# Adding the residual in the middle steps of the second product, longer last steps, and activations in DRAM by token quarters

## The chip, the cores and the metric

The kernel runs on one core of a Trainium2 chip, as one launch. The metric is the device time of that launch in microseconds (us). A core has TensorE (PE, matrix products; PEld is its weight load), VectorE (DVE), ScalarE (ACT), GpSimd (POOL) and SyncE (SP), which here issues every DMA, in one queue and in order. Each engine works through its own list of instructions in order; semaphores tie the lists together. SBUF is the on-chip memory with 128 partitions, PSUM holds the results of TensorE, and tensors in DRAM are reached by DMA only.

## The reference, cut to what matters

```python
D_MODEL = SEQ = 1024; D_FF = 4096; ALPHA = 2 ** 0.25

def reference(x, w_in, b_f, pool_w, pool_scale, w_out, ln1_g, ln1_b, w_mlp1, w_mlp2, ln2_g, ln2_b):
    mix = hybrid_mixer(x, w_in, b_f, pool_w, pool_scale, w_out)    # untouched by the change
    x = layer_norm(ALPHA * x + mix, ln1_g, ln1_b)                  # "x1" below
    hid = jnp.square(jax.nn.relu(x @ w_mlp1))                      # first product
    return layer_norm(ALPHA * x + hid @ w_mlp2, ln2_g, ln2_b)      # second product, residual, norm

def layer_norm(x, g, b):
    mu = jnp.mean(x, axis=-1, keepdims=True)
    var = jnp.mean(jnp.square(x - mu), axis=-1, keepdims=True)
    return (x - mu) * lax.rsqrt(var + 1e-5) * g + b
```

All values are float32. Each factor is split into a high and a low part (float32r), and a product takes three matmuls (high by high, high by low, low by high).

## The kernel before, in words

The mixer comes first, then `x1`: eight tiles of 128 tokens by 1024, normed by `norm` on VectorE and stored to `x1_dram`. Both products of the MLP then use the Strassen-Winograd scheme: with each matrix cut into two by two blocks, seven block products `p1` to `p7` stand for eight.

**First product.** Sixteen units (`class Unit`), each two blocks of 128 hidden columns. A unit runs its seven products, each 12 matmuls of 128x128 by 512, in the order p1, p2, p6, p5, p7, p3, p4; VectorE and ScalarE form the relu squares and the sums that the second product needs as its left factors, seven blocks with the names A12, A11, S1, S2, S3, S4, A22. `out` (L655) splits a block into high and low, and stores both to `hid_dram`, whose layout is `[unit, partition, high/low, 7 blocks, 512 tokens]`: a block lies there with its 512 tokens (of one half of the sequence) in a row.

**Second product.** The sixteen units are now the contraction. A step (`class Step`) takes one quarter `q = s % 4` of the 512 tokens of each half, and some consecutive units: step `s` takes the units s-3 to s that exist, so there are 19 steps, with 1, 2, 3, then thirteen times 4, then 3, 2, 1 units. Each step has seven products, each of three matmuls per unit. Its results are added (`into`, L863 to L869) to two tiles `y[q]` and `y[q + 4]` of 128 tokens by 1024 in SBUF, which stay there for all steps. Since each pair of weight tiles (`class Pair`, from `w2`) is used in four steps in a row, one pair comes in with each step: `load_f` (L780) and `load_g` (L784) load 512 KB each into slots of the tag "S" (three buffers of 4 KB a partition); `split_b`, `sums`, `split_t2`, `split_t13` and `split_t4b` make the seven right factors from them, in slots "B".

**Loads of the second product.** `load` (L846) brings the left factors of a step, a block pair at a time: 256 KB a unit for two blocks, 128 KB for A22. A partition's share of one block and one half (high or low) is 128 numbers, 512 bytes in a row. These land in slots "Q" and "A" (eleven of them turn over). `load_y` (L853) fills `y[q]` and `y[q + 4]` with the two tiles of `x1`, 512 KB each, in each of the first four steps; the first addition to a half of `y` then multiplies by ALPHA as it adds (L867, VectorE).

**Last steps.** From step 15 on, a step finishes its two tiles: `norm` with `by="pool"` has statistics on VectorE, the centring on ScalarE (L508) and the two operations with gamma and beta on GpSimd (L509, L512). In the last step, the first tile uses `by="both"` (L492 on VectorE, L511 on ScalarE, L512 on GpSimd), the second `by="vector"` (L492 and L503, stored half by half at L504).

**Order.** Units and steps stand in one chain. Between two neighbours, the products are interleaved by hand: p1 of the new one, p7 of the old, p2, p3 of the old, p6, p4 of the old, p5. `at(i, place, ...)` puts loads, splits and stores between these products, before product number `place`. The program's text gives priorities; the framework's scheduler then orders each engine's list and SP's queue by when a thing can run in its model, and makes an instruction wait where a buffer of its tag is still in use.

The PSUM banks: `k1` of a step is used in turn by p1, p6, p7 and p4, so each of these waits until `into` has read the one before.

Of the kernel before, what the change touches and what calls it, by code (L numbers as in the profile page):

```python
# [14 lines left out]
P = 128  # L15
S = 1024
# [20 lines left out]
def trunk(ctx, tc, xT, xn, wuqk, wvf, bf, poolw, pscale, wout, g1, b1, w1, w2, g2, b2, out):  # L37
# [418 lines left out]
    hid_dram = dr.tile([NF // 2, P, 2, 7, CH], F32, name="hid_dram")  # L456
    H = KT // 2
    VI = {b: i for i, b in enumerate(("A12", "A11", "S1", "S2", "S3", "S4", "A22"))}
# [15 lines left out]
    def norm(y, gam, bet, store, parts=(), res=None, by="vector"):  # L474

        cols = [slice(0, CH), slice(CH, D)]
        st = small([P, 4, 6], "bns", bufs=2)
        mv, rt = small([P, 2], "mv", bufs=2), small([P, 5], "rt", bufs=2)  # L480
        for i, c in enumerate(cols):
            if parts:
                nc.vector.scalar_tensor_tensor(y[:, c], res[:, c], ALPHA, parts[i], ALU.mult, ALU.add)
            nc.vector.bn_stats(st[:, i], y[:, c])
        nc.vector.bn_aggr(mv, st[:, :2])
        v, s, q, r, n = (rt[:, i : i + 1] for i in range(5))

        nc.scalar.activation(s, mv[:, 1:2], AF.Sqrt, bias=eps_sb, scale=0.25)
        nc.vector.tensor_scalar(v, mv[:, 1:2], EPS, 0.25, ALU.add, ALU.mult)

        def scaled(c):
            nc.vector.scalar_tensor_tensor(y[:, c], y[:, c], mv[:, 0:1], gam[:, c], ALU.subtract, ALU.mult)  # L492

        if by != "pool":
            scaled(cols[0])
        nc.vector.reciprocal(q, s)
        nc.vector.scalar_tensor_tensor(q, q, v, s, ALU.mult, ALU.add)
        nc.vector.reciprocal(r, q)
        if by != "pool":
            scaled(cols[1])  # L500
        if by == "vector":
            for c in cols:
                nc.vector.scalar_tensor_tensor(y[:, c], y[:, c], r, bet[:, c], ALU.mult, ALU.add)  # L503
                nc.sync.dma_start(store[:, c], y[:, c])  # L504
            return
        if by == "pool":
            nc.vector.tensor_scalar(n, mv[:, 0:1], r, -1.0, ALU.mult, ALU.mult)
            nc.scalar.activation(y, y, AF.Identity, scale=r, bias=n)  # L508
            nc.gpsimd.tensor_tensor(y, y, gam, ALU.mult)  # L509
        else:  # L510
            nc.scalar.mul(y, y, r)  # L511
        nc.gpsimd.tensor_tensor(y, y, bet, ALU.add)  # L512
        nc.sync.dma_start(store, y)
# [45 lines left out]
    class Unit:  # L559
# [69 lines left out]
        def p7(self):  # L629
            product(self.b1, self.v["T3"], "S3", False)  # L630

            self.rb = slot("A", [2, CH], F32)
            nc.vector.tensor_tensor(self.rb[:, 1], self.cc[:, 1], self.b1, ALU.subtract)

        def p3(self):
            product(self.b2, self.v["B22"], "S4", False)
            nc.vector.tensor_tensor(self.ra[:, 0], self.b2, self.cc[:, 0], ALU.subtract)
            nc.scalar.activation(self.ra, self.ra, AF.Relu)
            nc.scalar.activation(self.ra, self.ra, AF.Square)

        def p4(self):
            product(self.b1, self.v["T4"], "A22", False)
            nc.scalar.activation(self.rb[:, 0], self.b1, AF.Relu)
            nc.scalar.activation(self.rb[:, 1], self.rb[:, 1], AF.Relu)
            nc.scalar.activation(self.rb, self.rb, AF.Square)
            ra, rb = self.ra, self.rb
            self.sa, self.sb = slot("A", [2, CH], F32), slot("A", [2, CH], F32)
            nc.vector.tensor_tensor(self.sb[:, 0], ra[:, 1], rb[:, 0], ALU.subtract)
            nc.vector.tensor_tensor(self.sa[:, 0], rb[:, 0], rb[:, 1], ALU.subtract)

        def sums_s(self):
            nc.vector.tensor_tensor(self.sa[:, 1], self.sa[:, 0], self.ra[:, 1], ALU.subtract)
            nc.vector.tensor_tensor(self.sb[:, 1], self.ra[:, 0], self.sa[:, 1], ALU.add)

        def out(self, name, x):  # L655

            n, i = x.shape[1], VI[name]
            hi = slot("A", [n, CH])
            nc.scalar.copy(hi, x)  # L659
            nc.vector.tensor_tensor(x, x, hi.bitcast(F32), ALU.subtract)  # L660
            nc.sync.dma_start(hid_dram[self.u, :, 0, i : i + n], hi.bitcast(F32))
            nc.sync.dma_start(hid_dram[self.u, :, 1, i : i + n], x)

        def out_r(self):
            self.out("A12", self.ra)
            self.out("A22", self.rb[:, 1:2])
# [8 lines left out]
    for m in range(4):  # L675
# [13 lines left out]
        for t in (2 * m, 2 * m + 1):  # L689
# [18 lines left out]
            norm(xt, gam, bet, x1_dram[t], yp, xt)  # L708
# [116 lines left out]
    NS = NU + 3  # L825

    class Step:

        def __init__(self, s):
            self.s, self.q = s, s % 4
            self.us = [u for u in range(s - 3, s + 1) if 0 <= u < NU]
            self.first, self.final = s < 4, s >= NS - 4
            self.h = {}

        def load(self, names):

            n, i = len(names), VI[names[0]]
            per = 2 // n * 2 if n == 1 else 2  # L840
            qs = slice(self.q * P, (self.q + 1) * P)
            for a in range(0, len(self.us), per):
                h = slot("Q" if nh[0] % 11 < 8 else "A", [per, 2, n, P])
                nh[0] += 1
                for e, u in enumerate(self.us[a : a + per]):
# [163 lines left out]
```

## Time and profile before

| | |
|---|---|
| median of 3 runs | 1090.63 us (1089.4 to 1091.59) |
| profiled execution, its own time | 1088.95 us |
| its span, first to last instruction | 1087.1 us |
| mean granted TensorE clock | 0.979 |
| bytes moved by DMA | 202.62 MB, mean 186 GB/s |
| matmuls of the first product (L554) | from 420.8 us to about 737 us |
| matmuls of the second product (L859) | from 725.1 us to 1067.9 us |

The times of instructions and of stretches below are from the profiled execution, counted from its first instruction. A row of the windows view gives, for a stretch, the busy time of each engine with its number of instructions, the granted clock of TensorE (1.00 is full speed), the mean busy share of the 16 DMA engines (it can come out above 1, since the records of packets overlap a little) and the rate moved. In the timeline and the chain of waits, a row begins with start and duration; in brackets stands the idle time of the engine before it and what ended it. SPq is SP's queue: its rows are the issuing of a DMA, not the transfer.

### The profile page before, as it was taken

What the parts mean: (1) busy time and instruction counts of PE and PEld (TensorE: products, weight loads), DVE (VectorE), ACT (ScalarE), POOL (GpSimd) and SP (SyncE); (2) the same over time, 40 slices, a digit from 0 to 9 for tenths busy, and PEclk for the clock granted to TensorE, in tenths of its full rate; (3) what the DMA queues carried; (4) which work ended last, traced back from release to release, by engine and by line L of the source; (5) the groups of instructions that cost most, each with busy time, mean ns of one, the idle gap of its engine ahead of it and who ended that gap; (6) DMA issues with size and microseconds to landing.
All of it is one profiled execution on the core that took longest, in us unless ns stands there. A gap on an engine that the chain in (4) does not pass through costs nothing.

```text
span 1087.1 us, 14056 instructions
## 1 busy us (share of the span) xinstructions
PE 1029.6 (95%) x5006; PEld 850.3 (78%) x5006; DVE 776.3 (71%) x1315; ACT 493.9 (45%) x783; POOL 59.9 (6%) x77
## 2 busy tenths in 40 slices
PE   7999999999989999999999999995899999999992
PEld 7988788888768777788888888883688888888881
DVE  3576777777886889698887878786665655555378
ACT  3423565666772315477667666763221212222012
POOL 0000000000000021100000000000000000000046
PEclk9999999999999999999999999997799999999996
DMA  6303211111455522167766667599999888888732
GB/s 214 100 26 115 84 49 50 33 50 49 148 158 168 190 98 78 58 252 271 279 243 244 260 224 288 205 334 335 331 303 279 253 248 245 242 253 255 204 122 116
DMA packets 168181, 202.62 MB, mean 186 GB/s; under 512 B 9832, under 2 KB 131496, under 8 KB 168112
## 3 DMA queue, kind: packets, MB, share of 16 engines
q1 hardware_dynamic: 168112, 201.73, 56.8%
q8 instruction: 39, 0.64, 0.3%
q14 instruction: 30, 0.25, 0.1%
HBM read 130.32 MB, written 71.37 MB: 186 GB/s over the span
## 4 chain that ended last, share of the span: by engine, by line
PE 79%; DVE 10%; DMA 5%; ACT 3%; issue 2%; SPq 1%; DVEq 0%; ACTq 0%
PE s L859 15%; PE s L554 11%; PE pv L859 7%; PE mm L554 7%; PE pt L554 6%; PE pv L554 4%; PE pv L384 3%; PE mm L85 2%; PE mm L83 2%; PE mm L84 2%; PE pt L859 2%; PE mm L859 2%; PE s L85 2%; PE s L83 2%; PE s L84 2%
## 5 line engine op out<-in xcount | busy, mean ns | idle before, releaser
L71 ACT CAST B<-S 128x1024 fp32r<-128x1024 f32 (+1 forms) x94 | 80.5, 868 | 207.7 <-DMA S<-in_w_dram 80.7
L859 PE MATMUL s<-B,Q 128*128 128x512 f32 x564 | 139.2, 396 | 12.7 <-DMA Q<-hid_dram 12.7
L859 PEld LDWEIGHTS s<-B,Q 128*128 128x128 f32 x564 | 107.3, 191 | 36.6 <-issue 11.0
L554 PE MATMUL s<-B,Q 128*128 128x512 f32 x504 | 121.0, 393 | 0.7 <-ACT B L71 0.7
L72 DVE TENSOR_TENSOR B<-S,B 128x1024 fp32r<-128x1024 f32 (+1 forms) x94 | 92.8, 994 | 39.1 <-ACT B L71 38.9
L554 PEld LDWEIGHTS s<-B,Q 128*128 128x128 f32 x504 | 95.6, 190 | 21.5 <-ACT B L71 1.0
L71 ACT CAST Q<-S 128x1024 fp32r<-128x1024 f32 x53 | 55.6, 1050 | 62.7 <-DVE S L685 15.4
L72 DVE TENSOR_TENSOR Q<-S,Q 128x1024 fp32r<-128x1024 f32 x53 | 64.6, 1220 | 24.2 <-ACT Q L71 24.0
L554 PE MATMUL mm<-B,Q 128*128 128x512 f32 x324 | 77.6, 390 | 0.0
L859 PE MATMUL pv<-B,Q 128*128 128x512 f32 x279 | 70.8, 397 | 3.8 <-DVE A L867 1.4
L554 PEld LDWEIGHTS mm<-B,Q 128*128 128x128 f32 x324 | 60.8, 188 | 12.9 <-DVE Q L72 0.4
L554 PE MATMUL pt<-B,Q 128*128 128x512 f32 x288 | 68.7, 389 | 0.0
L660 DVE TENSOR_TENSOR A<-A,A 128x1024 f32<-128x1024 f32 (+1 forms) x64 | 67.0, 1084 | 0.2 <-ACT A L659 0.2
L384 PE MATMUL pv<-A,B 128*128 128x256 f32 x320 | 61.5, 297 | 5.0 <-ACT A L369 3.3
L859 PEld LDWEIGHTS pv<-B,Q 128*128 128x128 f32 x279 | 52.9, 190 | 16.8 <-DVE A L867 1.9
L384 PEld LDWEIGHTS pv<-A,B 128*128 128x128 f32 x320 | 49.1, 188 | 21.4 <-ACT A L369 9.9
L554 PEld LDWEIGHTS pt<-B,Q 128*128 128x128 f32 x288 | 54.1, 188 | 11.2
L659 ACT CAST A<-A 128x1024 fp32r<-128x1024 f32 x64 | 58.8, 942 | 6.9 <-DMA hid_dram<-A 2.6
L370 DVE TENSOR_TENSOR A<-pt,A 128x512 fp32r<-128x512 f32 (+1 forms) x80 | 49.2, 634 | 16.4 <-ACT A L369 15.8
L347 ACT ACTIVATE A<-A,nm 128x128 f32<-128x128 f32 (+3 forms) x64 | 49.8, 777 | 20.4 <-DVE nm L345 20.1
L859 PE MATMUL s<-B,A 128*128 128x512 f32 x204 | 53.3, 403 | 2.3 <-DVE A L869 2.3
L869 DVE TENSOR_TENSOR A<-A,s 128x512 f32<-128x512 f32 x47 | 32.0, 681 | 30.3 <-PE s L859 30.3
(353 smaller groups left out, 2125.2 us busy)
## 6 DMA issues: line engine op xcount, KB each, us to landing
hid_dram<-A SPq DMA_DIRECT2D x96, 512.0 KB
Q<-hid_dram SPq DMA_DIRECT2D x141, 256.0 KB
S<-in_w_dram SPq DMA_DIRECT2D x63, 512.0 KB
A<-hid_dram SPq DMA_DIRECT2D x51, 256.0 KB
hid_dram<-A SPq DMA_DIRECT2D x32, 256.0 KB
S<-in_wuqk_dram SPq DMA_DIRECT2D x12, 512.0 KB
Q<-hid_dram SPq DMA_DIRECT2D x47, 128.0 KB
A<-ncf_dram SPq DMA_DIRECT2D x8, 512.0 KB
```

What stands on the lines that cost most here:

```text
L71: nc.scalar.copy(hi, src)
L72: nc.vector.tensor_tensor(lo, src, hi.bitcast(F32), ALU.subtract)
L83: nc.tensor.matmul(dst, a[0], b[0], start=first, stop=False)
L84: nc.tensor.matmul(dst, a[0], b[1], start=False, stop=False)
L85: nc.tensor.matmul(dst, a[1], b[0], start=False, stop=last)
L347: nc.scalar.activation(pt[:, :nk], pt[:, :nk], AF.Exp, bias=nm, scale=-1.0, accum_out=rsum[h][:, i : i + 1])
L370: nc.vector.tensor_tensor(tt[:, 1, ev], tp[:, ev], tt[:, 0, ev].bitcast(F32), ALU.subtract)
L384: nc.tensor.matmul(ov, V[j][:, h].rearrange("p s d -> p (s d)"), tt[:, s, a:b], start=(j == 0 and s == 0), stop=(j == 2 * m + 1 and s == 1),)
L554: nc.tensor.matmul(dst, b[x][:, k], A[a][y][:, k], start=first and k == 0 and i == 0, stop=k == H - 1 and i == 2, skip_group_check=not first,)
L659: nc.scalar.copy(hi, x)
L660: nc.vector.tensor_tensor(x, x, hi.bitcast(F32), ALU.subtract)
L859: nc.tensor.matmul(dst, h[:, p_], w[q_], start=first and u == self.us[0] and j == 0, stop=u == self.us[-1] and j == 2, skip_group_check=no ...
```

## The change

The residual: `load_y` is gone. In the first four steps `room` only takes the two slots, and the first addition to a half of `y` becomes a copy from PSUM on ScalarE, with its sign (`nc.scalar.mul`). In each of the steps 4 to 11, `load_x` brings one tile of `x1` into a slot of the tag "S", and `add_x` adds ALPHA times it to `y` on VectorE.

The steps: there are still 19, but the units of the steps 12 to 18 are 9-11, 10-12, 11-13, 12-15, 12-15, 13-15 and 14-15, so 3, 3, 3, 4, 4, 3, 2 of them, where they were 4, 4, 4, 4, 3, 2, 1. The pairs 14 and 15 both come in for step 15.

DRAM: `hid_dram` keeps a pair of blocks as four token quarters, and in each quarter the 128 tokens of the one block, then those of the other; a partition's share of a load is then 1024 bytes in a row for the pairs, and still 512 for A22. The tiles of the first product have the shape [4, 2, 128] for that. A22 is split into a tile of its own and stored with one DMA instead of two.

The norms: the class `Norm` has the same operations in pieces. Statistics of a half are taken as soon as that half of `y` is finished; the tiles of steps 15 to 17 use ScalarE and GpSimd as before; in the last step the second tile goes on VectorE alone, and then the first tile's gamma and beta too, so GpSimd has nothing of that step.

```diff
-    hid_dram = dr.tile([NF // 2, P, 2, 7, CH], F32, name="hid_dram")
+    hid_dram = dr.tile([NF // 2, P, 2, 7 * CH], F32, name="hid_dram")
+    GROUPS = (("A12", "A11"), ("S1", "S2"), ("S3", "S4"), ("A22",))
+    AT = {g[0]: 2 * i * CH for i, g in enumerate(GROUPS)}
+    def quarters(a):
+        return a.rearrange("p (q t) -> p q t", q=4)
...
+        def centred(self):
+            self.root()
+            r, n = self.inverse(), self.rt[:, 4:5]
+            nc.vector.tensor_scalar(n, self.mv[:, 0:1], r, -1.0, ALU.mult, ALU.mult)
+            nc.scalar.activation(self.y, self.y, AF.Identity, scale=r, bias=n)
+        def affine(self, eng):
+            eng.tensor_tensor(self.y, self.y, self.gam, ALU.mult)
+            eng.tensor_tensor(self.y, self.y, self.bet, ALU.add)
+            nc.sync.dma_start(self.store, self.y)
...
-            self.ra = slot("A", [2, CH], F32)
-            nc.vector.tensor_tensor(self.ra[:, 1], b3, self.u1, ALU.add)
+            self.ra = slot("A", [4, 2, P], F32)
+            nc.vector.tensor_tensor(self.ra[:, :, 1], quarters(b3), quarters(self.u1), ALU.add)
...
         def out_r(self):
             self.out("A12", self.ra)
-            self.out("A22", self.rb[:, 1:2])
+            w = slot("A", [2, 4, P])
+            split(w[:, 0], w[:, 1], self.rb[:, :, 1])
+            nc.sync.dma_start(hid_dram[self.u, :, :, AT["A22"] :], w.bitcast(F32).rearrange("p h q t -> p h (q t)"))
...
-    NS = NU + 3
+    TAKES = [range(max(0, s - 3), s + 1) for s in range(12)]
+    TAKES += [range(9, 12), range(10, 13), range(11, 14), range(12, 16), range(12, 16), range(13, 16), range(14, 16)]
+    NS = len(TAKES)
+    FIRST = [min(s for s in range(NS) if u in TAKES[s]) for u in range(NU)]
...
-                    nc.sync.dma_start(h[:, e].bitcast(F32), hid_dram[u, :, :, i : i + n, qs])
+                    nc.sync.dma_start(h[:, e].bitcast(F32).rearrange("p h n t -> p h (n t)"), hid_dram[u, :, :, o : o + n * P])
...
-        def load_y(self):
+        def room(self):
             for t in (self.q, self.q + 4):
                 y[t] = slot("Q" if self.q == 0 else "A", [D], F32)
-                nc.sync.dma_start(y[t], x1_dram[t])
+        def load_x(self):
+            self.t = self.s - 4
+            self.xr = slot("S", [D], F32)
+            nc.sync.dma_start(self.xr, x1_dram[self.t])
+        def add_x(self):
+            nc.vector.scalar_tensor_tensor(y[self.t], self.xr, ALPHA, y[self.t], ALU.mult, ALU.add)
...
             if fresh and self.first:
-                nc.vector.scalar_tensor_tensor(dst, dst, ALPHA, src, ALU.mult, op)
+                nc.scalar.mul(dst, src, float(sign))
...
         def p4(self):
             self.prod(self.k1, "A22", "T4", False)
             self.into(1, c0, self.k1, True)
             if self.final:
-                norm(y[self.q + 4], *rows["gb"], out[self.q + 4], by="vector" if self.s == NS - 1 else "pool")
+                self.n1.stats(0)
+                if self.end:
+                    self.n1.on_vector()
+                    self.n0.affine(nc.vector)
+                else:
+                    self.n1.centred()
+                    self.n1.affine(nc.gpsimd)
...
-            if x.s < NU:
-                p = pairs[x.s]
-                at(i - 1, 0, p.load_f)
-                at(i - 1, 2, p.load_g)
...
+            for k, p in enumerate(p for p in pairs if FIRST[p.u] == x.s):
+                at(i - 1, 4 * k, p.load_f)
+                at(i - 1, 2 + 3 * k, p.load_g)
...
-                at(i - 1, 4, x.load_y)
+                at(i - 1, 4, x.room)
+            if 4 <= x.s < 12:
+                at(i - 1, 6, x.load_x)
+                at(i, 4, x.add_x)
```

More of the change, by code (lines that the diff above doesn't have):

```diff
@@ L472, in load_row @@
         return t
[L474 to L513, printed above, removed]
@@ new lines, in trunk, with __init__, stats, root @@
+    class Norm:
+        def __init__(self, y, gam, bet, store):
+            self.y, self.gam, self.bet, self.store = y, gam, bet, store
+            self.cols = [slice(0, CH), slice(CH, D)]
+            self.st = small([P, 2, 6], "bns", bufs=4)
+            self.mv, self.rt = small([P, 2], "mv", bufs=4), small([P, 5], "rt", bufs=4)
+        def stats(self, i):
+            nc.vector.bn_stats(self.st[:, i], self.y[:, self.cols[i]])
+        def root(self):
+            mv = self.mv
+            nc.vector.bn_aggr(mv, self.st)
+            v, s = self.rt[:, 0:1], self.rt[:, 1:2]
+            nc.scalar.activation(s, mv[:, 1:2], AF.Sqrt, bias=eps_sb, scale=0.25)
+            nc.vector.tensor_scalar(v, mv[:, 1:2], EPS, 0.25, ALU.add, ALU.mult)
+        def scaled(self, c):
+            y, gam = self.y, self.gam
+            nc.vector.scalar_tensor_tensor(y[:, c], y[:, c], self.mv[:, 0:1], gam[:, c], ALU.subtract, ALU.mult)
+        def inverse(self):
+            v, s, q, r = (self.rt[:, i : i + 1] for i in range(4))
+            nc.vector.reciprocal(q, s)
+            nc.vector.scalar_tensor_tensor(q, q, v, s, ALU.mult, ALU.add)
+            nc.vector.reciprocal(r, q)
+            return r
+        def on_vector(self):
+            y = self.y
+            self.root()
+            for c in self.cols:
+                self.scaled(c)
+            r = self.inverse()
+            for c in self.cols:
+                nc.vector.scalar_tensor_tensor(y[:, c], y[:, c], r, self.bet[:, c], ALU.mult, ALU.add)
+                nc.sync.dma_start(self.store[:, c], y[:, c])
+        def centred(self):
+            self.root()
+            r, n = self.inverse(), self.rt[:, 4:5]
[5 more added lines that the diff above has]
+            nc.sync.dma_start(self.store, self.y)
@@ L630, in p7 @@
             product(self.b1, self.v["T3"], "S3", False)
-            self.rb = slot("A", [2, CH], F32)
-            nc.vector.tensor_tensor(self.rb[:, 1], self.cc[:, 1], self.b1, ALU.subtract)
+            self.rb = slot("A", [4, 2, P], F32)
+            nc.vector.tensor_tensor(self.rb[:, :, 1], quarters(self.cc[:, 1]), quarters(self.b1), ALU.subtract)
         def p3(self):
             product(self.b2, self.v["B22"], "S4", False)
-            nc.vector.tensor_tensor(self.ra[:, 0], self.b2, self.cc[:, 0], ALU.subtract)
+            nc.vector.tensor_tensor(self.ra[:, :, 0], quarters(self.b2), quarters(self.cc[:, 0]), ALU.subtract)
             nc.scalar.activation(self.ra, self.ra, AF.Relu)
@@ L707, in trunk @@
                 x1_transposed(*last)
-            norm(xt, gam, bet, x1_dram[t], yp, xt)
+            nm = Norm(xt, gam, bet, x1_dram[t])
+            for i, c in enumerate(nm.cols):
+                nc.vector.scalar_tensor_tensor(xt[:, c], xt[:, c], ALPHA, yp[i], ALU.mult, ALU.add)
+                nm.stats(i)
+            nm.on_vector()
             last = (t, xt)
@@ L862, in prod, with into @@
                     )
-        def into(self, second, c, src, fresh, op=ALU.add):
+        def into(self, second, c, src, fresh, sign=1):
             dst = y[self.q + 4 * second][:, c]
             if fresh and self.first:
-                nc.vector.scalar_tensor_tensor(dst, dst, ALPHA, src, ALU.mult, op)
+                nc.scalar.mul(dst, src, float(sign))
             else:
-                tt(dst, dst, src, op)
+                tt(dst, dst, src, ALU.add if sign > 0 else ALU.subtract)
         def p1(self):
@@ L874, in p1 @@
             self.into(0, c0, self.k1, True)
+            if self.final:
+                self.n0, self.n1 = (Norm(y[t], *rows["gb"], out[t]) for t in (self.q, self.q + 4))
         def p2(self):
@@ L882, in p2 @@
                 self.into(0, c0, k3s[self.q], False)
+                self.n0.stats(0)
         def p6(self):
             self.prod(self.k1, "S2", "T2", False)
-            self.into(0, c1, self.k1, True, ALU.subtract)
+            self.into(0, c1, self.k1, True, -1)
         def p5(self):
@@ L894, in p7 @@
             self.prod(self.k1, "S3", "T3", False)
-            self.into(1, c1, self.k1, False, ALU.subtract)
+            self.into(1, c1, self.k1, False, -1)
+            if self.final:
+                self.n1.stats(1)
         def p3(self):
@@ L900, in p3 @@
             if self.final:
-                norm(y[self.q], *rows["gb"], out[self.q], by="both" if self.s == NS - 1 else "pool")
+                self.n0.stats(1)
+                self.n0.centred()
+                if not self.end:
+                    self.n0.affine(nc.gpsimd)
         def p4(self):
```

55 lines of the change are left out of this document (26 added, 29 removed).

## The prediction

> **What bounds the kernel now.** I read the page first, its 40 slices above all (27.2 us each).
>
> ```profile
> span 1087.1 us, 14056 instructions
> ...
> PE   7999999999989999999999999995899999999992
> ...
> PEclk9999999999999999999999999997799999999996
> ```
>
> TensorE is full nearly everywhere. What the change touches are the two places where it isn't after the first slices: slices 28 and 29 (about 735 to 790 us), where the granted clock falls too, and the last one. So I cut the span into stretches, and asked how many matmuls each had.
>
> ```profile
> 500.00:700.00 200.00, 200.00 (x884) 165.64 (x884) 165.34 (x204) 136.67 (x169) 0.00 (x0) 1.00 0.67 254
> 735.50:798.40 62.90, 46.38 (x166) 35.25 (x166) 40.36 (x58) 18.14 (x24) 0.00 (x0) 0.81 1.06 326
> 798.40:840.00 41.60, 41.60 (x184) 34.21 (x183) 23.74 (x34) 7.93 (x10) 0.00 (x0) 1.00 1.03 288
> 850.00:1000.00 150.00, 150.00 (x660) 123.59 (x659) 83.90 (x117) 31.10 (x39) 0.00 (x0) 1.00 0.84 246
> 1051.30:1067.90 16.60, 14.18 (x61) 10.76 (x59) 16.12 (x43) 4.38 (x7) 12.22 (x6) 1.00 0.21 86
> 1067.90:1087.10 19.20, 0.00 (x0) 0.00 (x0) 16.02 (x23) 3.40 (x5) 12.87 (x5) 0.54 0.30 117
> ```
>
> The chain of waits gives the pace of undisturbed matmuls and what held TensorE in the gap; the waits between 740 and 770 us and a cut of the clock go with it.
>
> ```profile
> 722.56 2.72 PE pt L554 x12
> ...
> 756.74 5.43 DMA S<-in_w_dram
> ```
> ```profile
> PE s L859 <- DMA Q<-hid_dram: 12.7, 3, 7.6
> ```
> ```profile
> 754.00:772.00 18.00, 10.41 (x23) 7.38 (x24) 7.56 (x11) 3.14 (x4) 0.00 (x0) 0.54 1.08 333
> ```
>
> Twelve matmuls in 2.72 us are 0.227 us each. The 166 of the stretch from 735.5 to 798.4 us (steps 0 to 3 of the second product) would take 37.6 us; it lasted 62.9, so 25.3 us are lost: 16.5 us with no matmul (62.9 - 46.4), and 8.8 us to matmuls that run long, beside a clock of 0.54 at the worst place. The DMA engines were busy all the time there (1.06), and TensorE waited for loads. From 798 us on they are still full, but ahead of TensorE, which stands nowhere. From 850 us (steps of four units) they have air again: 0.84. So the second place where time is lost is the end: 61 matmuls from 1051.3 to 1067.9 need 13.8 us of 16.6, and then 19.2 us pass with no matmul at all.
>
> **The change part by part: the gap at 735 us.** What fills the DMA engines there:
>
> ```profile
> DMA packets 22477, 20.54 MB, mean 326 GB/s; under 512 B 1010, under 2 KB 19673, under 8 KB 22475
> ...
> Q<-hid_dram SPq DMA_DIRECT2D x26, 256.0 KB
> A<-x_dram SPq DMA_DIRECT2D x6, 512.0 KB
> ...
> A<-hid_dram SPq DMA_DIRECT2D x9, 256.0 KB
> Q<-hid_dram SPq DMA_DIRECT2D x6, 128.0 KB
> ...
> A<-hid_dram SPq DMA_DIRECT2D x4, 128.0 KB
> ```
>
> Of 20.54 MB, 10.5 MB are loads of activations (35 of 0.262 and 10 of 0.131 MB), 3.15 MB are six tiles of x1, the rest (6.9 MB) weights and stores of the last units. What a MB costs I take from two calm stretches. From 500 to 700 us, where rows are long (stores and weights), 254 GB/s take 0.67: the engines would reach 379 GB/s, or 2.64 us a MB. From 850 to 1000 us:
>
> ```profile
> DMA packets 59885, 36.95 MB, mean 246 GB/s; under 512 B 2249, under 2 KB 57830, under 8 KB 59878
> ...
> S<-in_w_dram SPq DMA_DIRECT2D x16, 512.0 KB
> ```
>
> and, for the length of the long rows, the packets from 500 to 690 us:
>
> ```profile
> DMA packets 14304, 47.23 MB, mean 249 GB/s; under 512 B 1584, under 2 KB 1584, under 8 KB 14292
> ```
>
> From 850 us, 8.4 MB are weights, 22.1 us at that rate; the other 28.6 MB, activations in rows of 512 bytes, take what is left of 150 x 0.84 = 126 us, 103.9 us, or 3.63 us a MB (275 GB/s). As a check: 10.5 x 3.63 + 10.05 x 2.64 = 64.6 us for the gap, which lasted 62.9. So the gap is as long as its bytes, and the working can be inverted:
>
> - The six tiles of x1 leave: 3.15 x 2.64 = 8.3 us less.
> - The two tiles of step 0 were issued before 735.5 us, when TensorE wasn't waiting yet. Without them what follows lands up to 2.8 us (1.05 MB) sooner; between 0 and 2.8 I take the middle, 1.4, since nothing says how much of their queue was left.
> - Rows of 1024 bytes for 6/7 of the activations, 9.0 MB. The trace has no such rows. Bounds: 3.63 us a MB (no gain) and 2.64 (all, 8.9 us). If a row has a fixed cost, a MB costs c + k / length; with 512 bytes at 3.63 and some 3300 at 2.64 (47.23 MB in 14304 packets), k is 600 and 1024 bytes come to 3.05, nearer to the long rows. I take 0.58 x 9.0 = 5.2 us.
>
> The Trainium skill, "DMA: Bandwidth & Descriptors", section "Specifications", says that transfers of 512 bytes and more go at line rate. By that the third term would be nothing. The two rates above (275 and 379 GB/s) speak against it, but they mix reads and writes, so it stands among the rivals.
>
> Together 14.9 us; the gap shrinks to 48.0 us, with 37.6 as its floor. Bounds: 8.3 and 20.0.
>
> What else is moved there. The first additions go from VectorE to ScalarE:
>
> ```profile
> 721.13 0.58 ACT L622 COPY Q<-mm 128x512 f32<-128x512 f32 x1
> ```
>
> Sixteen copies of about 0.6 us: 9.6 us, on an engine with 18.1 of 62.9 us busy; VectorE, 40.4 busy, loses as many additions. Behind a late weight tile such a copy now waits in ScalarE's queue as the addition did in VectorE's. I put both at nothing; without the cover it would be one copy a product, 0.6 us, before the bank is free.
>
> **The steps 4 to 11.** Each gets a tile of x1 (0.52 MB) and a wide operation on VectorE. DMA: a step of 84 matmuls lasts 19.0 us and now moves 3.67 MB of activations and 1.05 of weights: 13.3 + 2.8 = 16.1 us. Afterwards 3.15 x 3.05 + 0.52 x 3.63 + 1.57 x 2.64 = 15.7 us; with no gain from rows, 17.5. Both fit into 19.0. VectorE has 83.9 of 150 us busy, 10.6 a step; `add_x` costs at most two of the 0.93 us rows of L492 quoted below. Nothing, as long as that air is there.
>
> The price could lie in the "S" slots: three, now for f, g and the tile. The rows around one step:
>
> ```profile
> 842.60 0.33 SPq L784 DMA_DIRECT2D S<-in_w_dram  x1
> ...
> 846.67 0.62 ACT L71 CAST B<-S 128x512 fp32r<-128x512 f32 x1 [3.07 <-DMA S<-in_w_dram]
> ...
> 847.96 0.68 DVE L72 TENSOR_TENSOR B<-S,B 128x512 fp32r<-128x512 f32 x1
> ...
> 852.18 1.23 DVE L72 TENSOR_TENSOR B<-S,B 128x1024 fp32r<-128x1024 f32 x1 [1.07 <-ACT B L71]
> ...
> 853.80 0.59 SPq L780 DMA_DIRECT2D S<-in_w_dram  x1
> ...
> 861.18 1.56 PE L859 MATMUL mm<-B,A 128*128 128x512 f32 x6
> ```
>
> `load_g` is issued at 842.6, as soon as f's slot is free; B21, made from it, is ready at 848.6 and used at 861.2: 12.5 us of slack. If the third slot goes to the tile, g waits in the worst case for `split_t4b`, which ends at 853.4: 11.2 us later, and still 1.3 us early. If the tile is added as soon as it lands, the delay is far less. I take nothing, and bound it by 0 and what the last rival gives.
>
> **First product and x1.** Same operations on as many elements in another order of addresses, one store fewer a unit. A unit lasts 19.0 us with TensorE full (200 of 200 us), VectorE at 83% and ScalarE at 68%. Even a tenth more on ten half operations of 0.7 us (0.7 us a unit) stays within the 3 us that VectorE has left. Nothing.
>
> **The end.** Longer last steps cost no matmul: the number is the same. Rows of the timeline:
>
> ```profile
> 1054.12 0.22 DVE L497 SCALAR_TENSOR_TENSOR rt<-rt 128x1 f32<-128x1 f32 x1
> ...
> 1055.46 0.69 DVE L484 BATCH_NORM_STATS2 bns<-Q 128x6 f32<-128x512 f32 x1
> ...
> 1056.15 2.40 POOL L509 TENSOR_TENSOR Q<-Q,S 128x1024 f32<-128x1024 f32 x1 [2.13 <-ACT Q L508]
> ...
> 1067.19 1.24 ACT L508 ACTIVATE A<-A,rt 128x1024 f32<-128x1024 f32 x1 [0.52 <-DVE rt L507]
> 1067.20 0.68 DVE L869 TENSOR_TENSOR A<-A,pv 128x512 f32<-128x512 f32 x1
> ...
> 1070.49 0.93 DVE L492 SCALAR_TENSOR_TENSOR A<-A,mv,S 128x512 f32<-128x512 f32 x1
> ...
> 1073.58 2.79 POOL L509 TENSOR_TENSOR A<-A,S 128x1024 f32<-128x1024 f32 x1
> ...
> 1074.09 2.29 DVE L497 SCALAR_TENSOR_TENSOR rt<-rt 128x1 f32<-128x1 f32 x1
> ...
> 1076.44 5.09 POOL L512 TENSOR_TENSOR A<-A,S 128x1024 f32<-128x1024 f32 x2
> ...
> 1077.33 4.75 DVE L492 SCALAR_TENSOR_TENSOR A<-A,mv,S 128x512 f32<-128x512 f32 x2
> ...
> 1082.64 1.42 DVE L503 SCALAR_TENSOR_TENSOR A<-A,rt,S 128x512 f32<-128x512 f32 x2
> ```
>
> Here an operation of VectorE with two operands in SBUF that starts beside GpSimd ends about when GpSimd's does: L497 takes 2.29 us instead of 0.22, the pair of L492 4.75 instead of 1.9. GpSimd ends at 1081.5, 13.6 us after the last matmul, VectorE at 1084.1, the span 3 us later.
>
> After the change the last step has 42 matmuls (9.5 us) instead of 21, so the norms of step 17 begin earlier against the end. Its second tile is complete 24 matmuls, 5.4 us, before the last matmul; then come an addition and statistics (0.7 each), seven small operations (0.2 each, as L497), and 1.25 us of ScalarE. GpSimd could start on it 1.3 us before the last matmul, but has the first tile (complete 39 matmuls, 8.8 us, before the end; two operations of 2.4) until about 0.3 us after it, with 0.2 us for handing over, and ends at +5.1. Until then VectorE can do what isn't held: additions and statistics. After +5.1 remain one L492 (0.95), the inverse (0.5), two L503 (1.4) and gamma and beta of the first tile (two operations of 1.2, as the 128x1024 row above): 5.3 us, so VectorE ends at +10.4. With a last store of 512 KB instead of 256 the 3 us become 3.7 (0.26 MB more at 2.64): the end is at +14.1 instead of +19.2, 5.1 us less. Of the 2.8 us lost before the last matmul I count half as gained, 1.4, as VectorE is still full there. Together 6.5.
>
> Bounds: VectorE's work from 8.8 us before the last matmul is seven additions and five statistics (8.4 us), three chains of small operations (1.1 each) and 6.6 us for the last two tiles, 18.3 us; if it waits for nothing it ends at +9.5, and with all 2.8 us back the gain is 8.8. If the pair 15, which now comes in together with 14, keeps TensorE waiting for the 5.4 us of the weight row above, it is 1.1.
>
> **Sum.** The profiled execution took 1088.95 us, 1.68 below the median of the runs, 1090.63. 1088.95 - 14.9 - 6.5 = 1067.6 us; put back on the median's scale, **1069 us**. Of a kernel of this length some 0.2% (2 us) can be told from no change.
>
> **The rivals.**
>
> *Rows of 1024 bytes gain nothing* (the skill's rule above): the gap shrinks by 9.7 us, 1069 + 5.2 = 1074 us. For it speaks that reads and writes may differ in rate; against it that the check of the gap's length came out with the two rates. 13%.
>
> *All of the gap goes*: the clock stays up once no wait is long, and the loads were late because SP stood with stores ahead of them, not for bytes. 25.3 instead of 14.9: 1059 us. The engines' 1.06 through the whole gap speaks against it. 10%.
>
> *The end stays as long*, because GpSimd, with four operations of 2.4 us from step 17, still ends last and VectorE's last operations queue behind it: 1069 + 6.5 = 1075 us. 12%.
>
> *The third slot holds SP.* `load_g` stands at the head of SP's queue until `split_t4b`, 11.2 us in each of the steps 4 to 11, and the loads of activations behind it come late. It decides where the delay passes 12.5 us, or the eleven slots of activations (seven are used a step, so 1.6 steps) run dry. At the gap one wait of SP cost up to 7.6 us of TensorE; with half of that, 3.8, in eight steps, 30 us are lost: 1099 us, slower. Against it: VectorE is free nearly half of the time there, so the tile's slot should be free early, and a step's need (15.7 of 19.0 us) is met. 10%, of which 2% end near no change.
>
> My forecast has 55%. The range is 1058 to 1081 us: below it takes in the second rival, above the third with a gap at its worse bound (1075 + 14.9 - 8.3 = 1081); only the last rival lies outside. Faster by over 0.2%: 0.55 + 0.13 + 0.10 + 0.12 = 0.90, less 0.01 for sums at the bad bounds: 0.89; the same 0.03; slower 0.08.
>
> **What would show it.** Right: the matmuls of steps 0 to 3 in about 48 us, the DMA engines full in them; a clock that dips less; no L853, and its loads spread over 150 us with TensorE full; activations at about 0.8 of the engines in steps 4 to 11; 14 us from the last matmul to the end, with the last L492-like operations still long beside GpSimd. Wrong: TensorE idle for weights in steps 4 to 11, a gap of over 55 us, or GpSimd busy to the end.

## The result, and the profile after

The changed kernel takes 1072.82 us (median of 4 runs, 1071.47 to 1073.28), against 1090.02 us before (4 runs beside it, 1088.03 to 1091.59). The ratio is 0.984, with an interval of 0.982 to 0.986: 17 us faster. The forecast was 1069 us. The profiled execution took 1073.26 us, so 15.7 us less than the profiled one of before, with a mean granted clock of 0.984. Its page:

```profile
span 1071.5 us, 14035 instructions
...
PE   8999999999989999899999999998699999999994
...
PEclk9999999999999999899999999998899999999998
...
DMA packets 118774, 202.62 MB, mean 189 GB/s; under 512 B 9576, under 2 KB 82088, under 8 KB 118704
...
q1 hardware_dynamic: 118704, 201.73, 54.3%
```

The same bytes go in 118,774 packets instead of 168,181, and cost 54.3% of the engines' time. The last line of before, with the share that belongs beside it:

```profile
q1 hardware_dynamic: 168112, 201.73, 56.8%
```

The weak places are still the slices 28 and 29 and the last one. The two have 8 and 6 tenths where they had 5 and 8, so 14 instead of 13 together, and the last one has 4 instead of 2; the clock is up in all three. The stretches of after that answer to those shown of before (busy time of each engine, clock, DMA share, GB/s):

```profile
723.00:733.60 10.60, 10.60 (x48) 8.80 (x47) 10.60 (x15) 7.77 (x12) 0.00 (x0) 1.00 0.74 272
733.60:789.90 56.30, 43.40 (x166) 34.43 (x165) 31.93 (x44) 24.09 (x35) 0.00 (x0) 0.85 0.97 327
850.00:1000.00 150.00, 150.00 (x661) 123.76 (x660) 95.32 (x131) 32.57 (x41) 0.00 (x0) 1.00 0.82 265
1057.05:1071.50 14.45, 0.00 (x0) 0.00 (x0) 10.66 (x20) 2.24 (x4) 5.34 (x3) 0.65 0.37 146
```

The span, 15.6 us shorter, splits at three marks: the end of the first product's last matmul (735.48 before, 733.56 after), the start of the 24 matmuls with which step 4 begins (798.41 and 789.89), and the last matmul's end (1067.86 and 1057.05).

| | before | after | less | forecast |
|---|---|---|---|---|
| up to the gap | 735.48 | 733.56 | 1.9 | 0 |
| the gap | 62.9 | 56.3 | 6.6 | 14.9 |
| step 4 to the last matmul | 269.45 | 267.16 | 2.3 | 1.4 |
| after the last matmul | 19.2 | 14.45 | 4.8 | 5.1 |

The end came as worked out, the gap gave less than half. The gap splits again at the matmul that follows its longest wait. Before:

```profile
735.50:759.40 23.90, 11.00 (x36) 7.69 (x36) 16.97 (x24) 8.33 (x11) 0.00 (x0) 0.77 0.98 333
759.40:798.40 39.00, 35.38 (x130) 27.56 (x131) 23.39 (x34) 9.81 (x13) 0.00 (x0) 0.83 1.11 322
```

And after:

```profile
733.60:759.16 25.56, 12.67 (x42) 9.27 (x40) 13.19 (x19) 11.42 (x17) 0.00 (x0) 0.77 0.95 339
759.16:789.88 30.72, 30.71 (x124) 25.14 (x125) 18.74 (x26) 12.67 (x19) 0.00 (x0) 0.92 0.99 316
```

At 0.227 us a matmul, the second part lost 9.5 us before (39.0 - 130 x 0.227) and loses 2.6 now; TensorE doesn't stand there any more. The first part lost 15.7 us before and loses 16.0 now: nothing was gained in it. What TensorE waits for in it, and the row of SP's own waits that goes with it (two waits, of which the one of 4.5 us lies in the gap):

```profile
PE s L895 <- DMA A<-hid_dram: 9.7, 1, 9.7
PE pv L895 <- ACT Q L903: 3.2, 1, 3.2
```
```profile
SPq L680 <- ACT A L677: 7.5, 2, 4.5
```

L680 is the store of a block of the last units, L677 the split that it waits for. The chain of waits of after tells the order (start, duration, what):

```profile
738.63 4.66 DMA Q<-hid_dram
743.31 1.05 ACT A L677
...
748.49 0.16 SPq L680
...
751.19 1.19 SPq L808
...
752.47 1.16 SPq L874
...
754.40 4.73 DMA A<-hid_dram
759.17 4.21 PE s L895 x9
```

And TensorE, ScalarE and SP in the timeline of the same stretch:

```profile
737.49 0.60 ACT L903 ACTIVATE Q<-pv 128x512 f32<-128x512 f32 x1
738.15 1.65 PE L895 MATMUL pv<-B,Q 128*128 128x512 f32 x3 [3.22 <-ACT Q L903]
...
742.82 0.60 ACT L903 ACTIVATE A<-s 128x512 f32<-128x512 f32 x1 [4.72 <-PE s L895]
743.31 1.04 ACT L677 CAST A<-A 128x1024 fp32r<-128x1024 f32 x1
...
746.89 4.25 SPq L680 DMA_DIRECT2D hid_dram<-A  x4
```

One thing stands behind another. A copy (L903, at 737.49) comes late on ScalarE, behind the relus and squares of unit 15, and TensorE waits 3.22 us for it; the 15 matmuls behind this wait take 6.2 us. The next copy waits 4.72 us for a product among them; the split of a block of unit 15 (L677) stands behind that copy on ScalarE; its stores stand behind the split on SP (L680); and the next loads (L874) stand behind the stores, until 752.47. The chain puts a load (738.63) ahead of the split, but that load landed at 743.29, after the copy had begun at 742.82, so it isn't what the copy waited for. Before, a load does stand at the head: TensorE waits for it until 744.00, and behind its products follow the addition (L867) and the split's subtraction (L660) on VectorE, the store (L662) and the next loads (L846):

```profile
737.27 6.68 DMA Q<-hid_dram
...
744.00 1.65 PE s L859 x3
...
751.37 0.04 DVE A L867
...
751.98 1.22 DVE A L660
...
753.81 0.23 SPq L662
...
754.09 1.21 SPq L846
```

SP comes to those loads 18.6 us after the gap's start before, and 18.9 after, whether four tiles of x1 were issued ahead of them or none.

### The profile page after: what moved, and what is told of

The parts are those of the page before. It is cut to its first block, busy times and chain, and to the rows that moved or that the text cites. A ratio compares the mean times of both kernels' runs of the same rounds, so it can differ in the third digit from the quotient of the medians.

```text
span 1071.5 us, 14035 instructions
## 1 busy us (share of the span) xinstructions
PE 1026.8 (96%) x5006; PEld 850.3 (79%) x5006; DVE 772.5 (72%) x1308; ACT 500.9 (47%) x799; POOL 57.6 (5%) x76
## 2 busy tenths in 40 slices
DMA packets 118774, 202.62 MB, mean 189 GB/s; under 512 B 9576, under 2 KB 82088, under 8 KB 118704
## 3 DMA queue, kind: packets, MB, share of 16 engines
q1 hardware_dynamic: 118704, 201.73, 54.3%
## 4 chain that ended last, share of the span: by engine, by line
PE 79%; DVE 9%; DMA 4%; ACT 4%; issue 2%; SPq 1%; DVEq 0%; ACTq 0%
PE s L895 15%; PE s L573 11%; PE pv L895 8%; PE mm L573 6%; PE pt L573 6%; PE pv L573 4%; PE pv L384 3%; PE mm L85 2%; DMA S<-rin_dram 2%; PE mm L83 2%; PE mm L84 2%; PE mm L895 2%; PE pt L895 2%; PE s L83 2%; PE s L85 2%
## 5 line engine op out<-in xcount | busy, mean ns | idle before, releaser
L895 PE MATMUL s<-B,Q 128*128 128x512 f32 x558 | 135.8, 393 | 0.4 <-DVE A L905 0.4
L72 DVE TENSOR_TENSOR B<-S,B 128x1024 fp32r<-128x1024 f32 (+1 forms) x94 | 92.7, 993 | 46.5 <-ACT B L71 46.2
L895 PEld LDWEIGHTS s<-B,Q 128*128 128x128 f32 x558 | 105.4, 189 | 23.7 <-DVE A L905 0.9
L573 PE MATMUL s<-B,Q 128*128 128x512 f32 x504 | 121.5, 395 | 0.4 <-ACT B L71 0.4
L72 DVE TENSOR_TENSOR Q<-S,Q 128x1024 fp32r<-128x1024 f32 x53 | 64.6, 1220 | 23.8 <-ACT Q L71 23.6
L573 PE MATMUL pt<-B,Q 128*128 128x512 f32 x288 | 68.7, 389 | 0.0
L678 DVE TENSOR_TENSOR A<-A,A 128x1024 f32<-128x1024 f32 x48 | 57.0, 1217 | 2.9 <-ACT A L677 2.9
L895 PEld LDWEIGHTS s<-B,A 128*128 128x128 f32 x210 | 40.6, 194 | 19.0 <-DMA A<-hid_dram 10.1
L83 PE MATMUL mm<-B,B 128*128 128x512 f32 x120 | 51.7, 430 | 0.0
```

The source lines that it names most:

```text
L72: nc.vector.tensor_tensor(lo, src, hi.bitcast(F32), ALU.subtract)
L83: nc.tensor.matmul(dst, a[0], b[0], start=first, stop=False)
L573: nc.tensor.matmul(dst, b[x][:, k], A[a][y][:, k], start=first and k == 0 and i == 0, stop=k == H - 1 and i == 2, skip_group_check=not first,)
L895: nc.tensor.matmul(dst, h[:, p_], w[q_], start=first and u == self.us[0] and j == 0, stop=u == self.us[-1] and j == 2, skip_group_check=no ...
```

## The experiments

Each kernel is the changed one with an edit; the first three are reached from it by undoing the other two parts. The first theory was that of the forecast (the gap is as long as its bytes); against it stood that SP's queue, the slots of the loads, or the new copies on ScalarE hold it. The length of the gap serves as the measure beside the time: the first matmul of the second product, ahead of which the code of most of these kernels is the same, came between 722.4 and 726.6 us in their profiles, and this scatter moves the whole time.

**The layout alone.**

```diff
-    hid_dram = dr.tile([NF // 2, P, 2, 7, CH], F32, name="hid_dram")
+    hid_dram = dr.tile([NF // 2, P, 2, 7 * CH], F32, name="hid_dram")
...
-                    nc.sync.dma_start(h[:, e].bitcast(F32), hid_dram[u, :, :, i : i + n, qs])
+                    nc.sync.dma_start(h[:, e].bitcast(F32).rearrange("p h n t -> p h (n t)"), hid_dram[u, :, :, o : o + n * P])
```

> The kernel before with only the DRAM layout by token quarters (and A22 in a tile of its own); residual, steps and norms as before. Theory 'bytes' (the gap at 735 us is as long as what the DMA engines move in it): the gap falls by the 5.2 us of the prediction, or 6 to 6.5 with the rate that the changed kernel shows for rows of 1024 bytes; total about 1084 us. Theory 'queues' (the gap is set by where loads stand in SP's queue, behind stores that wait for VectorE and ScalarE): cheaper rows shorten only the landing of a load that is already late; 0 to 3 us, total 1087 to 1090 us. Both: busy share of the DMA engines from 850 to 1000 us falls from 0.84 to about 0.74.

1086.38 us against 1088.58; ratio 0.998 (0.997 to 0.999). The gap lasts 63.3 us. Windows of this kernel:

```profile
734.09:797.38 63.29, 44.89 (x167) 34.46 (x166) 40.01 (x58) 18.04 (x24) 0.00 (x0) 0.84 1.00 344
...
850.00:1000.00 150.00, 150.00 (x659) 123.50 (x658) 84.00 (x117) 31.08 (x39) 0.00 (x0) 1.00 0.77 245
```

From 850 us the engines need 0.77 instead of 0.84 for the same rate, so rows of 1024 bytes are cheaper. The gap is no shorter: 344 GB/s instead of 326 moved more bytes in it, loads for later steps. The 2 us of the whole time lie elsewhere. So for the gap the theory of the queues holds, and that of the bytes doesn't.

**The residual alone.**

```diff
-                nc.sync.dma_start(y[t], x1_dram[t])
...
-                nc.vector.scalar_tensor_tensor(dst, dst, ALPHA, src, ALU.mult, op)
+                nc.scalar.mul(dst, src, float(sign))
...
+            if 4 <= x.s < 12:
+                at(i - 1, 6, x.load_x)
+                at(i, 4, x.add_x)
```

> The kernel before with only the residual moved: no load of x1 in steps 0 to 3, first additions are copies on ScalarE, one tile of x1 in each of the steps 4 to 11. Theory 'bytes': 8.3 to 11 us less, total 1079 to 1082 us. Theory 'queues': the loads of x1 leave SP's queue, but the stores stay ahead of the rest, and the copies queue on ScalarE behind the relu and square of the last unit; 2 to 6 us less, total 1084 to 1088 us, with a wait of TensorE for L903 of about 3 us.

1083.87 us; 0.995 (0.994 to 0.997). The gap:

```profile
735.29:791.67 56.38, 43.71 (x166) 34.20 (x166) 31.98 (x44) 24.04 (x35) 0.00 (x0) 0.85 1.06 320
```

56.4 us, as in the full change: the residual alone gives all that the gap gave, less than the 8.3 us of its bytes.

**The longer last steps and the norms alone.**

```diff
+    TAKES += [range(9, 12), range(10, 13), range(11, 14), range(12, 16), range(12, 16), range(13, 16), range(14, 16)]
...
-                norm(y[self.q + 4], *rows["gb"], out[self.q + 4], by="vector" if self.s == NS - 1 else "pool")
+                self.n1.stats(0)
```

> The kernel before with only the longer last steps and the norms in halves; layout and residual as before. Both theories: the gap is as before (62 to 63 us), and the end gives what the changed kernel shows there, 7.1 us (4.75 after the last matmul, 2.4 before it); total 1083 us. If the end's gain depends on cheaper loads, less.

1081.67 us; 0.993 (0.991 to 0.995). The gap is 63.8 us; after the last matmul 14.47 us pass, as in the full change. The three parts alone come to 0.0136 of the time, together they give 0.0159; the intervals don't tell these apart.

**The first copies on VectorE.**

```diff
-                nc.scalar.mul(dst, src, float(sign))
+                nc.vector.tensor_scalar(dst, src, float(sign), None, ALU.mult)
```

> The changed kernel with the sixteen first copies on VectorE instead of ScalarE, nothing else. Theory 'bytes': no change, 1072 to 1074 us, since the loads bind. Theory 'queues': the 3.2 us for which TensorE waited for L903 go, and the half clock after it; 3 to 6 us less, total 1067 to 1070 us; if VectorE is just as late there, 0 to 2 us.

1074.2 us; 0.987 (0.985 to 0.988), so no better than the full change: of the two cases that the theory of the queues allowed, it is that of a VectorE as late as ScalarE. The gap is 55.5 us. The row of its waits that takes the place of the ScalarE one:

```profile
PE pv L895 <- DVE Q L903: 2.6, 1, 2.6
```

TensorE waits nearly as long for the copy in VectorE's queue. The first split on ScalarE (L677), now with no copy ahead of it, begins at 737.05 instead of 743.31. But the longest wait stays (8.1 us), and SP's loads come at 751.18 instead of 752.47: L678, the other half of the split, now stands behind a copy on VectorE.

**The stores of the units 14 and 15 issued by GpSimd.**

```diff
-                nc.sync.dma_start(hid_dram
+                (nc.gpsimd if self.u >= 14 else nc.sync).dma_start(hid_dram
```

> The changed kernel with the stores of the last two units (14 and 15) to DRAM issued from GpSimd's queue instead of SP's; GpSimd has nothing else to do there. Theory 'queues': SP no longer stands at stores that wait for VectorE and ScalarE, so the loads of steps 1 and 2 are issued some 6 to 8 us earlier, and the 9.7 us wait of TensorE at 750 us falls to 2 to 5 us; total 1064 to 1069 us. Theory 'bytes': as many bytes go over the same DMA engines; the gap stays within 2 us, total 1071 to 1075 us. If GpSimd is slow to issue, and the stores hold the slots that the next tiles wait for, slower.

1070.11 us; 0.983 (0.980 to 0.985). Its gap and two rows of its waits:

```profile
735.45:787.87 52.42, 44.05 (x166) 33.89 (x166) 32.01 (x44) 24.11 (x35) 3.89 (x7) 0.84 0.98 347
```
```profile
PE s L895 <- DMA A<-hid_dram: 5.4, 3, 3.6
PE s L895 <- ACT A L903: 2.6, 1, 2.6
```

With nearly the same bytes (18.2 MB against 18.4) the gap is 3.9 us shorter, and the wait of 9.7 us is down to 5.4 in three pieces, a little short of what the theory of the queues had (2 to 5). By the whole time the gain over the full change isn't certain.

**The loads of the steps 0 to 3 issued by GpSimd.**

```diff
-                    nc.sync.dma_start(h[:, e]
+                    (nc.gpsimd if self.s < 4 else nc.sync).dma_start(h[:, e]
```

> The changed kernel with the loads of activations of the steps 0 to 3 issued from GpSimd's queue instead of SP's. The counterpart of the run before: now the loads pass the stores. Theory 'queues': gap shorter by 4 to 9 us, total 1064 to 1069 us. Theory 'bytes': within 2 us, total 1071 to 1075 us.

1079.96 us; 0.992 (0.989 to 0.995): worse than the full change. The gap:

```profile
732.75:791.73 58.98, 46.12 (x167) 35.02 (x166) 30.19 (x42) 24.20 (x35) 23.01 (x32) 0.86 0.93 330
```

GpSimd is busy for 23.01 us with issuing 32 DMAs, 0.72 each; the engines' share falls to 0.93. The theory of the queues had 4 to 9 us less here, and missed. TensorE's waits for loads are down to 3.9 us, but it waits 4.0 us for a copy (L903) and 4.6 us for an addition (L905): other waits have come in the place of the one that went.

**No residual at all.**

```diff
-            if 4 <= x.s < 12:
-                at(i - 1, 6, x.load_x)
-                at(i, 4, x.add_x)
```

> The changed kernel without load_x and add_x: the residual is left out of the output. It tells what the eight tiles cost in the steps 4 to 11. The prediction put them at nothing: no difference beyond 1 us, total 1072 to 1074 us. If the third 'S' slot or the DMA engines bind there, it is faster by what they cost, up to 8 us.

1074.57 us; 0.987 (0.985 to 0.989). From step 4 to the last matmul it takes 267.16 us, the same as the full change.

**The full change with the old layout.**

> The changed kernel with the DRAM layout of before (rows of 512 bytes, A22 stored in two DMAs). The layout alone gave 2 us. Theory 'bytes': the gap is longer by 5 to 6 us, total 1078 us. Theory 'queues': 1 to 3 us longer, total 1074 to 1076 us. If steps 4 to 11 need the cheaper rows for the added tile (16.1 + 1.4 = 17.5 of 19.0 us of the DMA engines), TensorE shows waits there.

1075.75 us; 0.988 (0.986 to 0.990). Its windows:

```profile
734.83:791.17 56.34, 43.29 (x166) 34.34 (x166) 31.88 (x44) 23.97 (x35) 0.00 (x0) 0.85 1.04 320
790.00:945.00 155.00, 155.00 (x680) 127.32 (x679) 92.45 (x126) 32.84 (x42) 0.00 (x0) 1.00 0.98 282
```

The gap is the same, 56.3 us. In the middle steps the engines are full without the new layout (0.98), and TensorE still doesn't wait.

**The first fifteen tiles of activations all in slots "Q".** This tells whether the slots "A", which the last unit's blocks hold, keep the loads waiting.

```diff
-    slot("Q" if nh[0] % 11 < 8 else "A", [per, 2, n, P])
+    slot("Q" if nh[0] < 7 or (nh[0] - 7) % 11 < 8 else "A", [per, 2, n, P])
```

> The changed kernel in which the first 15 tiles of activations (up to step 2) are all put into slots 'Q', and the turn of 8 in 'Q' and 3 in 'A' begins after them; before, tiles 9 to 11 (of step 2) go into slots 'A', which the last unit's blocks hold until they are stored. Theory 'slots': TensorE's 9.7 us wait at 750 us is for a load that can't be issued before these stores have landed; with slots 'Q' it goes ahead of them, and the gap, from the last matmul of the first product to step 4, falls from 56.3 us to 46 to 51. Theory 'SP's order' alone: the stores still stand ahead of the load, gap 54 to 57 us. Theory 'bytes': 55 to 57 us. Whole times differ by up to 3 us from what happens ahead of the first product, so the gap is the measure.

1072.74 us; 0.986 (0.984 to 0.987). The gap is 54.3 us, where the theory of the slots had 46 to 51, and the wait only changes its name:

```profile
PE s L895 <- DMA Q<-hid_dram: 8.3, 1, 8.3
```

**Both, and all three.** The next has the slots and the stores on GpSimd; the one behind it the copies on VectorE as well.

> As the run before, with the stores of units 14 and 15 from GpSimd's queue too. Stores alone on GpSimd gave a gap of 52.4 us. Theory 'slots': what was left there (5.4 us for activations in slots 'A') goes, gap 42 to 47 us, total 1062 to 1067 us. If 'SP's order' was all, as with the stores alone: 51 to 53 us.

1070.87 us; 0.985 (0.983 to 0.986); the gap is 51.7 us, as with the stores on GpSimd alone (52.4), so the slots hold nothing that shows.

> As the run before, with the first copies on VectorE. If ScalarE's list is what is left (2.6 us of waiting for L903 with the stores on GpSimd), gap 40 to 44 us, 37.6 being the matmuls alone; if VectorE is as late as ScalarE, as with the copies alone on VectorE (55.5 instead of 56.3 us), no difference to the run before.

1078.85 us; 0.992 (0.990 to 0.993); the gap is 59.2 us. Its waits, and the load in its chain that they are for:

```profile
PE s L895 <- DMA Q<-hid_dram: 11.7, 2, 7.8
```
```profile
743.84 12.57 DMA Q<-hid_dram
```

The three don't add up, and neither of the two cases expected has come. The load goes out 8 us earlier than those after the stores in the full change, but lands only after 12.57 us, where the two in that chain take 4.7. While it is under way (743.84 to 756.41), GpSimd's stores take 70.2% of the engines' time and SP's loads 34.6%, 3.61 MB against 1.48: loads that have passed the stores still share the engines with them. With the copies left on ScalarE the shares over the same time are nearly these (68.7 and 35.3%), but the loads were out sooner: here SP stands 7.6 us, until 737.54, at a weight load (L804) that waits for a split on VectorE (L72). That split begins at 725.20 with the copies on ScalarE; here VectorE makes a copy at 725.64, and the split begins at 736.25.

**No stores of unit 15**, the rest as with the stores on GpSimd.

```diff
+                if self.u < 15:
...
-    hid_dram[u, :, :, o : o + n * P]
+    hid_dram[min(u, 14), :, :, o : o + n * P]
```

> As the run with the stores of units 14 and 15 from GpSimd (gap 52.4 us), but the stores of unit 15 are left out, and its activations are read from unit 14's place, so the output isn't the reference's; all splits stay. SP's order is the same; what goes is 3.67 MB in the gap and the hold of unit 15's blocks on the slots 'A'. Theory 'bytes': at 2.64 us a MB 9.7 us less, gap 42 to 44 us. Theory 'order and waits': the wait for loads into slots 'A' (5.4 us) shrinks and the rest stays, gap 47 to 50 us. If neither matters: 52 us, and what is left is the lists of VectorE and ScalarE and the clock.

1062.36 us (2 runs); 0.976 (0.973 to 0.980). The gap is 44.3 us. In two stretches, cut at the end of the last longer wait:

```profile
735.90:746.20 10.30, 7.40 (x31) 5.13 (x29) 8.59 (x13) 9.60 (x14) 0.00 (x0) 0.97 1.05 398
746.20:780.18 33.98, 33.94 (x136) 27.54 (x137) 23.46 (x32) 14.51 (x22) 0.00 (x0) 0.91 0.97 313
```

31 matmuls are done in the first 10.3 us, and then no wait is left. The longest wait of the gap has gone with the stores. This is what the theory of the bytes had (42 to 44 us), and not that of order and waits (47 to 50). The run takes away the stores' bytes and their hold on the slots at once, and doesn't tell the two apart.

The two parts of the gap in all kernels that have one long wait near 758 us, cut at the matmul behind it (with the stores on GpSimd, behind the last of three waits for loads):

| kernel | first part, us | second part, us |
|---|---|---|
| before | 23.9 | 39.0 |
| layout alone | 24.0 | 39.3 |
| last steps alone | 25.0 | 38.7 |
| residual alone | 25.4 | 31.0 |
| old layout, rest changed | 25.8 | 30.6 |
| full change | 25.6 | 30.7 |
| no residual | 24.4 | 30.8 |
| copies on VectorE | 24.7 | 30.8 |
| first loads in "Q" | 23.7 | 30.6 |
| stores on GpSimd | 21.9 | 30.5 |

## Why the prediction was partly right

**The gap: the term of x1 was nearly right, its place wasn't asked for.** In the table above, the second part is 38.7 to 39.3 us with x1 in the first steps and 30.5 to 31.0 us without: about 8.2 us, of which 1.4 are six matmuls that now come ahead of the cut. So 6.9 us less is lost (9.5 to 2.6), where six tiles had been put at 8.3. That the copies on ScalarE do this is ruled out by the run with them on VectorE (30.8); whether it is the tiles' bytes or SP's time for issuing them wasn't tried. With the residual moved and SP issuing the stores, the first part is 23.7 to 25.8 us, against 23.9 to 25.0 with x1 in the first steps.

**The step that failed** is "So the gap is as long as its bytes, and the working can be inverted". The gap gave 6.6 us, less than the 8.3 given as its lower bound, and at 56.3 us it shows one of the prediction's own signs of being wrong (over 55 us). The check behind the step (64.6 against 62.9) holds for any stretch in which the engines are full, whatever the bytes are for. The gap of the changed kernel moved 18.4 MB at 327 GB/s, before 20.5 MB at 326: the rate is the same, and the 2.15 MB less are the 6.6 us (2.15 / 0.327). Six tiles of x1 were 3.15 MB, so about 1 MB of room was filled with other transfers. The engines' share was 0.99 in the shortest gap (44.3 us) and 1.05 in the longest (63.8 us); it doesn't say which bytes TensorE waits for. It is an average, too: from 749 to 750 us before, and from 744 to 745 us after, the engines were busy for only 0.02 and 0.07 of the time, at the end of the time for which SP stood at a store that waited for its split (4.6 us before, 4.5 after). In the first part TensorE waited for the load behind unit 15's stores in SP's queue. That the stores hold it is shown by two runs: issued by GpSimd, they cost 3.9 us less; left out (3.67 MB, 9.7 us at 2.64), another 8.1. Each gap is from one profile: the six kernels with the residual moved and all DMAs issued by SP have 54.3 to 56.4 us, the two in which GpSimd issues the stores and ScalarE makes the copies have 52.4 and 51.7. So the order in SP's queue is worth some 2 to 4 us by itself; the larger part goes only with the stores themselves, and there their bytes may well count. The path through the copy and the split is read from the rows, and no run cut it whole: the copy on VectorE stands ahead of the same split's other half.

**The two tiles of step 0** (1.4 us) gave nothing that the first part shows. Ahead of the gap the engines' share fell from 0.97 to 0.74, and VectorE was busy for 10.60 of 10.60 us: the freed time of the engines was left unused.

**Rows of 1024 bytes** were sized well and credited in the wrong place. By the whole program, the engines were busy for 617.5 us before (56.8% of 1087.1) and 581.8 after (54.3% of 1071.5). The 35.7 us less, over 50.3 MB of loads of pairs (16 units, 4 quarters, 3 pairs of 0.262 MB), are 0.71 us a MB, where 0.58 had been estimated; the layout alone against before gives 0.53 (591.0 us), the full change against the one with the old layout 0.73 (618.5 us). The Trainium skill, "DMA: Bandwidth & Descriptors", section "Specifications", has transfers of 512 bytes and more at line rate; the share at equal GB/s (0.84 against 0.77) differs from that. Its consequence, no shorter gap, came true for another reason: TensorE's long wait wasn't for the length of those transfers. By the whole times the layout is worth 2.1 us alone, and 4.5 us beside the other parts (0.988 against 0.984). Where these arise isn't settled: of the 2.3 us between the two profiled spans with the old and the new layout, 1.0 lie between step 4 and the last matmul, and 1.3 are the start of the second product, within its scatter.

**The copies on ScalarE**: "I put both at nothing" held for the time, not for the waits. TensorE waits 3.2 us for a copy, and 2.6 us with the copies in VectorE's queue, so moving them back didn't help.

**Steps 4 to 11** were right: nothing. Without x1 they take the same 267.16 us up to the last matmul. The slot that was feared, in the timeline of the changed kernel:

```profile
850.80 1.23 DVE L889 SCALAR_TENSOR_TENSOR A<-S,A 128x1024 f32<-128x1024 f32 x1
...
852.05 0.34 SPq L804 DMA_DIRECT2D S<-in_w_dram  x1
...
853.19 0.33 SPq L808 DMA_DIRECT2D S<-in_w_dram  x1
...
859.16 0.69 DVE L72 TENSOR_TENSOR B<-S,B 128x512 fp32r<-128x512 f32 x1
```

`load_f` (L804) goes out as soon as `add_x` (L889) has ended, some 7 us later against its step than before. `load_g` (L808) follows 0.6 us after p2 begins at 852.60, before 0.5 us after it; the block made last from it is ready at 859.85, and its product starts at 871.87, 12.0 us later.

**The end** was forecast at +14.1 us and came at +14.45. In the timeline:

```profile
1059.96 2.86 POOL L531 TENSOR_TENSOR A<-A,S 128x1024 f32<-128x1024 f32 x1
...
1060.62 2.75 DVE L502 SCALAR_TENSOR_TENSOR A<-A,mv,S 128x512 f32<-128x512 f32 x1
...
1064.05 1.41 DVE L519 SCALAR_TENSOR_TENSOR A<-A,rt,S 128x512 f32<-128x512 f32 x2
...
1065.38 1.22 DVE L530 TENSOR_TENSOR A<-A,S 128x1024 f32<-128x1024 f32 x1
1066.63 1.22 DVE L531 TENSOR_TENSOR A<-A,S 128x1024 f32<-128x1024 f32 x1
1067.88 0.33 SPq L532 DMA_DIRECT2D out_dram<-A  x1
```

GpSimd ends at +5.8 (forecast +5.1), VectorE at +10.8 (+10.4), and the one L502 that starts beside GpSimd lasts 2.75 us instead of 0.73 and ends 0.55 us after it. Then come the operations that had been listed.

**The rivals.** "Rows of 1024 bytes gain nothing" (1074) was right for the gap; the time lies between it and the forecast. "All of the gap goes" named the wait of the first part, "SP stood with stores ahead of them", but this change doesn't touch it; the 1.06 that was held against it was no argument. "The end stays as long" fell with GpSimd's end at +5.8, and "the third slot holds SP" with the rows above.

**The sum**: 6.6 instead of 14.9 in the gap, 7.1 instead of 6.5 at the end, and 1.9 ahead of the gap, which is no more than the scatter there. That the time came within 4 us of the forecast is in part luck: of the 8.3 us that the gap fell short, 1.9 came back as this scatter.

## What to carry to other kernels

That the DMA engines are full in a stretch doesn't make it as long as its bytes: ask which load the waiting engine needs, what stands ahead of it in its queue, and what that waits for in turn. Here more bytes moved behind that load left the gap as long as it was (21.8 MB in 63.3 us with the layout alone, 20.5 in 62.9 before). Cut a gap at its longest wait before costing an edit, and give each part its own bound. Where a queue takes both the stores of one stage and the first loads of the next, look for a path that runs through both.

## What the runs showed of the hardware

Issuing a DMA isn't free. On SP a weight load (L808) takes 0.33 us in the middle steps and 0.47 to 1.19 in the gap; the loads of activations take 0.52 to 1.30 us there (1.16 at 752.47), and the stores mostly 1.1. On GpSimd a load of activations takes 0.72 us and a store 0.53. And a wait costs more than its length: the nine matmuls behind the wait of 9.68 us took 4.21 us, 0.47 each instead of 0.227, which is 2.2 of the 2.6 us that the second part of the gap still loses.
